# One short row of biases in DRAM, three output blocks at once on the arriving input, and dummy products in front

## The chip, the cores and the metric

The kernel runs on one core of one Trainium2 chip. The metric is the time of one execution on the device, in microseconds, lower is better; a kernel's time is the median of its runs. TensorE (PE in the profile) multiplies matrices, VectorE (DVE), ScalarE (ACT) and GpSimd (POOL) do the rest, SyncE (SP) issues most transfers.

## The reference

A trunk of two layers on x of 256 tokens by 2048 features, all in float32. Each layer is a mixer and a feed-forward part, each behind an rmsnorm and added to x.

```python
def swa_sink_attention(q, k, v, sinks, rel_bias):        # layer 0, 8 heads, window 128
    mask, bias = banded_mask_bias(rel_bias, A_WINDOW, nb)   # bias = rel_bias[t5_bucket(dist)]
    logits = einsum('bnqgrd,bnkgd->bgrnqk', qb, kb) * SCALE + bias
    ...
def nsa_attention(...):                                   # layer 1, 8 heads
    ...
    ls = einsum('bqgrd,bgqkd->bgrqk', qi, k_g) * SCALE + bias_s     # selected blocks
    lw = einsum('bqgrd,bkgd->bgrqk', qi, kwi) * SCALE + bias_w      # window 512
```

Beside them layer 0 has a forgetting attention and layer 1 a gated delta net. The bias of a query and a key depends on their distance alone: with 256 tokens each head has one row of at most 384 values per mask, read at another offset for each query.

## The kernel before

Nearly all of the time goes into products of weights with the activations. A weight is split into a high part `wh` (ACT, L168) and a remainder `wl` (DVE or POOL, L169); the activations are kept the same way in `xhl` (`split_x`: ACT at L385, DVE at L386, which multiply by the gain vector `vec`). A block of 128 output features (`f_job`) is 16 pairs of products, one per 128 input features: `wh` with 512 columns (L305) and `wl` with 256 (L306), summed in one PSUM bank. `v_job` gives token-major output, three products per input block and token block (L342 to L344).

Weights arrive as 1 MB loads into three buffers `wf`, issued by SP (L151); each load is cut into two pieces of 8 input blocks. `run` splits two pieces ahead of the products. The fragments of a split are issued in `hook`, which is called after every second pair; the same hook advances the side work, generators that say with `yield n` after how many hooks they go on. So the order of every engine's instructions is fixed by the count of hooks. An output block is taken out of PSUM (`fsum`: a copy at L448, an add at L451, then a product on POOL at L400) once the norm is known (`norm["ready"]`); `room(n)` holds the next job back until at most n results wait for it.

Layer 0 runs these jobs: two key blocks (k0, k1), query blocks q0 to q2, the token-major job V0 (264 columns), q3 to q7, two token-major jobs V1 of 512 columns, then 16 blocks for the other attention, then 32 half blocks for the output projection. `boot` issues the input x (four loads of 512 KB, `hT`), the first weights in two halves of 512 KB and a second load; it splits the input and the first two pieces. `first_gen` squares the input and sums it (L1412 on DVE, L1414 on ACT, L1416 on POOL, L1419 and L1421 on DVE), `norm_gen` turns that into the norm.

`bias_gen` makes the biases of all heads as 8 rows of 384 values with one product (L539), adds a mask in two versions (`brow`, L543) and writes each version 128 times into DRAM, one copy per query, with a row step of 385 (L547); head h then reads a skewed 128x256 table from it (`load_bias`, L555). `a_gen` runs the eight heads of the first attention: it waits for the query block, for V0 and for `state["bias"]`, loads the bias of head 0, waits 8 hooks, and from then on loads each head's bias one head ahead. `head_gen` (L567 to L606) issues the logits, the bias add with the maximum (L577, L578), the exponentials, transposes (L597 to L599) and the last product. `nsa_gen` in layer 1 does the same with three heads side by side, and loads the bias at the start of each head.

Of the kernel before, what the change touches and what calls it, by code (L numbers as in the profile page):

```python
# [48 lines left out]
WS = 3  # L49

# ---------------------------------------------------------------- shape-only constants
# [20 lines left out]
def _consts():  # L72
    p = np.arange(128)
    i64 = np.arange(64)
    j = np.arange(T)
    f = np.float32
    ident = np.eye(128, dtype=f)
    tri = (p[:, None] <= p[None, :]).astype(f)
    causal = np.where(j[None, :] <= 128 + p[:, None], 0.0, NEG).astype(f)
    y = np.arange(384)  # L80
    dist = 255 - y
    onehot = (np.arange(32)[:, None] == _t5_bucket(dist)[None, :]).astype(f)
    mask_a = np.where((dist >= 0) & (dist < 128), 0.0, NEG).astype(f)[None].repeat(8, 0)
    mask_c = np.where(dist >= 0, 0.0, NEG).astype(f)[None].repeat(8, 0)
    c0, o0 = _pack([("ident", ident)])
    c1, o1 = _pack([("tri", tri), ("causal", causal)])
    cb, ob = _pack([("onehot", onehot), ("mask_a", mask_a), ("mask_c", mask_c)])
    pj = p % 64
    blk = (p[:, None] // 64) == (p[None, :] // 64)
    lv, lvt = [], []  # L90
    for s in (1, 2, 4, 8, 16, 32):
        a, b = pj[:, None], i64[None, :]
        same = (a // (2 * s)) == (b // (2 * s))
        lv.append((same & (a % (2 * s) < s) & (b % (2 * s) >= s)).astype(f))
        lvt.append((same & (a % (2 * s) >= s) & (b % (2 * s) < s)).astype(f))
# [30 lines left out]
def trunk(ctx, tc, a, out):  # L126
# [16 lines left out]
    # ------------------------------------------------------------ weight stream  # L143
# [4 lines left out]
    def issue_load(l):  # L148
        src, n = loads[l]
        t = tmp.tile([128, 2048], F32, tag="wf", name="wf", bufs=3)  # L150
        nc.sync.dma_start(t[:, :n], src)  # L151
        wf_tiles[l] = t

    def split(i):
        pc = pieces[i]
        t = wf_tiles[pc["load"]]
        w = t[:, pc["off"]:pc["off"] + pc["n"]]
# [78 lines left out]
    def room(n):  # L236
        """at most n results wait for the norm."""
        while len(pending) > n:
            if norm["ready"]:
                flush()  # L240
            else:
                step_sides()

    def run():
        while state["i"] < len(pieces):
# [8 lines left out]
            if i < 2:  # L254
                settle()
# [6 lines left out]
            if pc["after"]:  # L262
                pending.append(pc["after"])
                flush()
# [11 lines left out]
    def f_job(src, nk, rhs, evac, pre=None, key=None, tag=None, one=False):  # L276
        """128 output features: psum[:, :256] + psum[:, 256:] is the product of src with rhs."""
# [39 lines left out]
    def v_job(src, ncol, xs, evac, pre=None):  # L317
        """token-major output [128 tokens, ncol] for the two token blocks."""
# [34 lines left out]
    # ------------------------------------------------------------ constants  # L353
# [26 lines left out]
    # ------------------------------------------------------------ norms  # L380
# [24 lines left out]
    def rsqrt(y, v, n, it=3):  # L405
        """y = v ** -0.5 on a [128, n] tile."""
# [66 lines left out]
    def to_out(k):  # L473
        """the last residual: its gained value goes to the output buffer, to be scaled by the norm."""
# [34 lines left out]
    def softplus(x, n, name):  # L509
        """log(1 + exp(x)) on a [128, n] tile."""  # L510
# [18 lines left out]
    # ------------------------------------------------------------ bias rows  # L529
# [4 lines left out]
    scr = [dram.tile([8, 128 * 385], F32, name=f"scr{q}") for q in range(2)]  # L534

    def bias_gen():
        yield 6
# [6 lines left out]
        for q in range(2):  # L544
            yield 4
            r = scr[q]
            nc.scalar.dma_start(bass.AP(tensor=r.tensor, offset=r.offset, ap=[[128 * 385, 8], [385, 128], [1, 384]]),  # L547
                                brow[q][:, None, :].to_broadcast([8, 128, 384]))
            yield 16
            state["bias"] = True  # L550

    def load_bias(q, h, tag):
        t = tmp.tile([128, T], F32, tag=tag, name="bias", bufs=1)
        r = scr[q]
        nc.scalar.dma_start(t, bass.AP(tensor=r.tensor, offset=r.offset + h * 128 * 385 + 127,  # L555
                                      ap=[[384, 128], [1, T]]))
        return t

    # ------------------------------------------------------------ attention of one head, two query blocks
# [3 lines left out]
    def head_gen(h, tags, u, q, k, v, add1, add0, oT, extra=None, sink=None):  # L563
        """softmax attention of head h; q, k: [128 d, 256]; v: two [128 keys, 128 d] blocks."""
# [44 lines left out]
    # ------------------------------------------------------------ layer 0 mixer  # L609
    def even_mixer():  # L610
# [76 lines left out]
        def a_gen():  # L687
            for h in range(8):
# [5 lines left out]
                if h < 7:  # L694
# [4 lines left out]
                                    bias, bias[:, 128:], oA[:, h], sink=sinks[:, h:h + 1])  # L699
# [22 lines left out]
        blk = iter(range(26))  # L722
        for g in range(2):
            f_job(wF[next(blk)], 16, x, ev_k(g))
        for h in range(8):
# [19 lines left out]
    # ------------------------------------------------------------ feed-forward  # L745
# [57 lines left out]
    def start_norm(scaled=False):  # L803
        def f():
            norm["ready"] = False
            side(norm_gen(scaled))
        return f
# [10 lines left out]
    # ------------------------------------------------------------ layer 1 mixer  # L818
    def odd_mixer():
# [100 lines left out]
        # ---- compressed keys and values  # L920
# [73 lines left out]
        # ---- sparse attention  # L994
        def nsa_gen(u, tag, tE, tP, tC, tB):
# [4 lines left out]
            while heads:  # L1000
# [9 lines left out]
                for qb in range(2):  # L1010
# [5 lines left out]
                    add = [bias[:, T - n:], bias[:, T - n:]]  # L1016
# [48 lines left out]
        # ---- gated delta net: head pairs, chunks of 64 tokens, both heads side by side on the partitions  # L1065
# [62 lines left out]
        def inv_gen(p, ta, tb):  # L1128
# [78 lines left out]
            def part(t, h, s):  # L1207
                """columns j of [128, 4, n] with j // s % 2 == h; h None: all of a [128, 4, 32] result."""
# [113 lines left out]
        # ---- jobs  # L1322
# [79 lines left out]
    # ------------------------------------------------------------ the two layers  # L1402
    late = [(c0, a["c0"]), (vec[:, nv:], a["vec"][:, nv:])]
    sqs = [big("t8_0", [128, 8, T], name="sqs"), big("t8_1", [128, 8, T], name="sqs")]

    def first_gen():
        f = lambda t: t.rearrange("p a t -> p (a t)")
        s = [f(sqs[q // 2][:, 4 * (q % 2):4 * (q % 2) + 4]) for q in range(4)]
        for q in range(4):
            h = f(hT[:, 4 * q:4 * q + 4])  # L1410
            if q % 2:
                V.tensor_mul(s[q], h, h)  # L1412
            else:
                A.activation(s[q], h, AF.Square)  # L1414
            if q % 2:
                G.tensor_tensor(s[q - 1], s[q - 1], s[q], op=ALU.add)  # L1416
            yield S1
        yield S2
        V.tensor_add(s[0], s[0], s[2])  # L1419
        yield 2  # L1420
# [3 lines left out]
        yield W0  # L1424
        acc["n"] = KT

    def boot(gi):
        """the input, the first weights and their parts, in the order of their use."""
        src, n = loads[0]
        wf_tiles[0] = t = tmp.tile([128, 2048], F32, tag="wf", name="wf", bufs=3)  # L1430
        state["nl"] = 1
        h = n // 2

        def lx(q):
            nc.sync.dma_start(hT[:, 4 * q:4 * q + 4], a["x"][:, 4 * q:4 * q + 4])

        def sx(q):
            for k in range(4 * q, 4 * q + 4):
                split_x(k, gi)

        lx(0)
        nc.sync.dma_start(t[:, :h], src[:, :h])
        lx(1)
        lx(2)
        nc.sync.dma_start(t[:, h:n], src[:, h:n])
        lx(3)
        issue_load(1)
        state["nl"] = 2
        for d, s in late:
            nc.sync.dma_start(d, s)  # L1450
        sx(0)
        split(0)
        settle()
        sx(1)
        sx(2)
        split(1)
        settle()
        sx(3)
# [4 lines left out]
    start_norm(True)()  # L1463
# [33 lines left out]
def _fblk(w):  # L1497
    """[K, N] -> [N / 128, 128, K / 128, 128], partitions first."""
# [66 lines left out]
```

## Time and profile before

| | |
|---|---|
| time, median of 3 runs | 2418.19 us (2416.05 to 2419.87) |
| profiled execution, span of core 0 | 2420.8 us |
| its time outside the span | not given; the span is 2.6 us over the median |
| TensorE busy | 2351.2 us, 97% |
| DVE, ACT, POOL busy | 66%, 55%, 27% |
| DMA | 425.00 MB, mean 176 GB/s |

TensorE is busy when a product is in its pipeline; how fast it goes depends on the clock that it is granted (PEclk), which has two levels, 1.2 and 2.4 GHz, shown as 0.50 and 1.00. Idle time of another engine counts only where TensorE waits for it.

### The profile page before, as it was taken

What the parts mean: (1) busy time and instruction counts of PE and PEld (TensorE: products, weight loads), DVE (VectorE), ACT (ScalarE), POOL (GpSimd) and SP (SyncE); (2) the same over time, 40 slices, a digit from 0 to 9 for tenths busy, and PEclk for the clock granted to TensorE, in tenths of its full rate; (3) what the DMA queues carried; (4) which work ended last, traced back from release to release, by engine and by line L of the source; (5) the groups of instructions that cost most, each with busy time, mean ns of one, the idle gap of its engine ahead of it and who ended that gap; (6) DMA issues with size and microseconds to landing.
All of it is one profiled execution on the core that took longest, in us unless ns stands there. A gap on an engine that the chain in (4) does not pass through costs nothing.

```text
span 2420.8 us, 40042 instructions
## 1 busy us (share of the span) xinstructions
PE 2351.2 (97%) x14374; PEld 2032.6 (84%) x14374; DVE 1595.0 (66%) x3454; ACT 1337.5 (55%) x3377; POOL 660.1 (27%) x926
## 2 busy tenths in 40 slices
PE   7799999999999999999999999999999999999997
PEld 5688888888888888888777777887888888888887
DVE  6457687666656666667887756778666655666654
ACT  4355566555545555555655445666555544555553
POOL 1223353111121111233444433345111121111132
PEclk9899999999999999999999999999999999999999
DMA  7554355555556555555433454345555556555554
GB/s 202 166 186 152 119 173 191 184 193 190 178 189 207 192 184 194 177 190 190 165 123 112 151 182 174 105 151 191 192 188 194 168 189 201 192 190 192 176 192 137
DMA packets 74358, 425.00 MB, mean 176 GB/s; under 512 B 8336, under 2 KB 12944, under 8 KB 31792
## 3 DMA queue, kind: packets, MB, share of 16 engines
q1 hardware_dynamic: 68544, 415.14, 50.2%
q10 hardware_dynamic: 5616, 7.32, 1.6%
q8 instruction: 113, 1.85, 0.3%
q14 instruction: 85, 0.70, 0.1%
HBM read 417.18 MB, written 5.24 MB: 174 GB/s over the span
## 4 chain that ended last, share of the span: by engine, by line
PE 83%; DVE 4%; issue 4%; POOL 4%; DMA 3%; ACT 2%; POOLq 0%; SPq 0%; DVEq 0%; ACTq 0%
PE mm L305 49%; PE mm L306 25%; POOL wl L169 2%; DVE wl L169 1%; DMA wf<-in_w_evF_dram 1%; PE s L1205 1%; DMA bias<-scr 1%; PE mm L342 1%; PE mm L343 1%; PE mm L344 1%; ACT wh L168 1%; DMA wf<-in_w_evV_dram 1%; POOL acc L403 1%; POOL hT L460 1%; PE s L1058 1%
## 5 line engine op out<-in xcount | busy, mean ns | idle before, releaser
L169 DVE TENSOR_TENSOR wl<-wf,wh 128x512 fp32r<-128x512 f32 (+4 forms) x1833 | 1105.6, 625 | 686.0 <-ACT wh L168 672.2
L305 PE MATMUL mm<-xhl,wh 128*128 128x512 f32 x3968 | 1418.6, 398 | 21.9 <-ACT wh L168 17.9
L168 ACT CAST wh<-wf 128x512 fp32r<-128x512 f32 (+2 forms) x2064 | 964.1, 510 | 423.1 <-PE mm L305 338.9
L306 PE MATMUL mm<-xhl,wl 128*128 128x256 f32 x3968 | 1124.0, 283 | 4.7 <-DVE wl L169 4.7
L305 PEld LDWEIGHTS mm<-xhl,wh 128*128 128x128 f32 x3968 | 751.3, 189 | 192.6 <-ACT wh L168 19.1
L306 PEld LDWEIGHTS mm<-xhl,wl 128*128 128x128 f32 x3968 | 756.2, 191 | 9.3 <-DVE wl L169 7.1
L305 PE MATMUL mm<-hid,wh 128*128 128x512 f32 x1386 | 482.1, 392 | 0.0
L306 PE MATMUL mm<-hid,wl 128*128 128x256 f32 x1386 | 388.5, 280 | 0.0
L400 POOL TENSOR_TENSOR gp<-ta,rbc 128x256 f32<-128x256 f32 x112 | 116.4, 1039 | 716.6 <-DVE ta L451 704.9
L305 PEld LDWEIGHTS mm<-hid,wh 128*128 128x128 f32 x1386 | 260.1, 188 | 58.4 <-DVE hid L507 1.2
L306 PEld LDWEIGHTS mm<-hid,wl 128*128 128x128 f32 x1386 | 260.7, 188 | 0.0
L448 ACT COPY tb<-mm 128x256 f32<-128x256 f32 x287 | 106.6, 372 | 265.0 <-PE mm L306 237.9
L169 POOL TENSOR_TENSOR wl<-wf,wh 128x256 fp32r<-128x256 f32 (+3 forms) x231 | 187.3, 812 | 172.9 <-ACT wh L168 154.7
L400 POOL TENSOR_TENSOR u<-u,cv 128x256 f32<-128x256 f32 x88 | 65.3, 742 | 212.5 <-ACT cv L783 212.5
L451 DVE TENSOR_TENSOR ta<-mm,tb 128x256 f32<-128x256 f32 x287 | 119.6, 417 | 1.7 <-ACT tb L448 1.7
L460 POOL TENSOR_TENSOR hT<-hT,ta 128x256 f32<-128x256 f32 x91 | 72.4, 796 | 81.6 <-DVE ta L451 64.1
L459 POOL TENSOR_TENSOR ta<-ta,rbc 128x256 f32<-128x256 f32 x39 | 38.2, 980 | 178.8 <-DVE ta L451 178.8
L403 POOL TENSOR_TENSOR acc<-acc,sq 128x256 f32<-128x256 f32 x59 | 52.3, 886 | 58.3 <-ACT sq L395 58.3
L783 ACT ACTIVATE cv<-cv 128x256 f32<-128x256 f32 x88 | 36.8, 419 | 55.5 <-DVE cv L781 55.5
L767 DVE TENSOR_TENSOR u<-mm,tb 128x256 f32<-128x256 f32 x88 | 37.5, 426 | 39.2 <-ACT tb L765 39.2
L342 PE MATMUL mm<-wh,xhl 128*128 128x512 f32 (+3 forms) x160 | 54.6, 341 | 6.4 <-ACT wh L168 6.4
L344 PE MATMUL mm<-wl,xhl 128*128 128x512 f32 (+3 forms) x160 | 54.1, 338 | 0.0
(353 smaller groups left out, 2048.5 us busy)
## 6 DMA issues: line engine op xcount, KB each, us to landing
wf<-in_w_up_dram SPq DMA_DIRECT2D x176, 1024.0 KB, 4.8
wf<-in_w_dn_dram SPq DMA_DIRECT2D x64, 1024.0 KB, 4.9
wf<-in_w_odF_dram SPq DMA_DIRECT2D x48, 1024.0 KB, 4.9
wf<-in_w_evF_dram SPq DMA_DIRECT2D x25, 1024.0 KB, 4.9
wf<-in_w_dn_dram SPq DMA_DIRECT2D x64, 384.0 KB, 3.1
wf<-in_w_evO_dram SPq DMA_DIRECT2D x32, 512.0 KB, 3.6
wf<-in_w_odO_dram SPq DMA_DIRECT2D x32, 512.0 KB, 3.6
wf<-in_w_evV_dram SPq DMA_DIRECT2D x8, 1024.0 KB, 4.9
```

Source lines behind the costliest of these rows:

```text
L168: A.copy(wh[:, c], w[:, c])
L169: e.tensor_tensor(wl[:, c], w[:, c], wh[:, c].bitcast(F32), op=ALU.subtract)
L305: P.matmul(ps, wh[:, c], xb.rearrange("p a t -> p (a t)"), start=k == 0, stop=False)
L306: P.matmul(ps[:, 256:512], wl[:, c], xb[:, 0, :], start=False, stop=k == nk - 1)
L342: P.matmul(ps, xh, wh[:, c], start=k == 0, stop=False)
L344: P.matmul(ps, xh, wl[:, c], start=False, stop=k == KT - 1)
L400: G.tensor_tensor(out, x, y, op=ALU.mult)
L403: G.tensor_tensor(out, x, y, op=ALU.add)
L448: A.copy(tb, ps[:, T:2 * T])
L451: V.tensor_tensor(t, ps[:, :T], tb, op=ALU.add)
L459: e.tensor_tensor(t, t, R["bc"], op=ALU.mult)
L460: e.tensor_tensor(hT[:, k], hT[:, k], t, op=ALU.add)
```

## The change

The bias rows are made in reverse order (`dist[::-1]`) and written once per version, 8 x 384 values. A head's load reads 128 overlapping rows of 256 values, each one value further on, and the bias is read backwards by DVE (`last_keys`, a step of -1). `bias_gen` starts at hook 34 instead of 6, and `state["bias"]` is set after both writes.

The first three blocks, k0, k1 and q0, are computed together (`boot_job`): eight pieces, each of two input blocks times three output blocks, in three PSUM banks. Input and weights come in five steps of x and the three blocks' weights (first two of 256 and 384 KB, then three of 512 and 768 KB); the fourth chunk of weights has a buffer of its own (`wf3`). Each piece splits its two input blocks and three weight parts, the middle one's remainder on POOL, two pieces ahead. There is a hook after every two pairs, so 24 in these jobs, as before.

`first_gen` now squares two quarters of the input on POOL (hooks 9 and 14), one on ACT and one on DVE, and adds on DVE alone. The norm waits 3 and 6 hooks where it waited 4 and 8. Nine products of `ones` with itself stand ahead of everything on TensorE. `room` now flushes and advances the side work in every round.

```diff
+WARM = 9
     dist = 255 - y
+    dist = dist[::-1]
 def issue_load(l):
     src, n = loads[l]
+        if callable(src):
+            wf_tiles[l] = src()
+            return
 def split(i):
+        if "parts" in pc:
+            ...
+            for k in pc["rows"]:
+                frags.append(lambda k=k: split_x(k, 0))
+            for o, c, n, e in pc["parts"]:
+                def piece(o=o, c=c, n=n, e=e):
+                    A.copy(wh[:, c:c + n], t[:, o:o + n])
+                    e.tensor_tensor(wl[:, c:c + n], t[:, o:o + n], wh[:, c:c + n].bitcast(F32), op=ALU.subtract)
+                frags.append(piece)
 def room(n):
         while len(pending) > n:
-            if norm["ready"]:
-                flush()
-            else:
-                step_sides()
+            flush()
+            step_sides()
 def run():
-            if i < 2:
-                settle()
+    def boot_job(src, evacs, rhs, bring):
+        box = {}
+        nb = len(evacs)
+        for c in range(4):
+            loads.append((lambda c=c: bring(c), nb * 512))
+            for q in range(2):
+                def mm(wh, wl, c=c, q=q):
+                    if c == q == 0:
+                        box["ps"] = [psm.tile([128, 512], F32, tag="mm", name="mm") for _ in range(nb)]
+                    for j in range(nb):
+                        ps = box["ps"][j]
+                        for r in range(2):
+                            k = 4 * c + 2 * q + r
+                            w = slice((2 * j + r) * 128, (2 * j + r + 1) * 128)
+                            xb = rhs(k)
+                            P.matmul(ps, wh[:, w], xb.rearrange("p a t -> p (a t)"), start=k == 0, stop=False)
+                            P.matmul(ps[:, 256:512], wl[:, w], xb[:, 0, :], start=False, stop=k == KT - 1)
+                        hook()
+                last = c == 3 and q == 1
+                add_piece(len(loads) - 1, 0, nb * 256, mm,
+                          [lambda j=j: start(evacs[j], box["ps"][j], None) for j in range(nb)] if last else None)
+                pieces[-1]["rows"] = range(4 * c + 2 * q, 4 * c + 2 * q + 2)
+                pieces[-1]["parts"] = [(j * 512 + q * 256, j * 256, 256, G if j == 1 else V) for j in range(nb)]
-    scr = [dram.tile([8, 128 * 385], F32, name=f"scr{q}") for q in range(2)]
+    scr = [dram.tile([8, 384], F32, name=f"scr{q}") for q in range(2)]
 def bias_gen():
-        yield 6
+        yield 34
         for q in range(2):
             yield 4
-            nc.scalar.dma_start(bass.AP(tensor=r.tensor, offset=r.offset, ap=[[128 * 385, 8], [385, 128], [1, 384]]),
-                                brow[q][:, None, :].to_broadcast([8, 128, 384]))
-            yield 16
-            state["bias"] = True
+            nc.scalar.dma_start(scr[q], brow[q])
+        yield 16
+        state["bias"] = True
 def load_bias(q, h, tag):
-        nc.scalar.dma_start(t, bass.AP(tensor=r.tensor, offset=r.offset + h * 128 * 385 + 127,
-                                      ap=[[384, 128], [1, T]]))
+        nc.scalar.dma_start(t, bass.AP(tensor=r.tensor, offset=r.offset + h * 384 + 1, ap=[[1, 128], [1, T]]))
+    def last_keys(t, n):
+        return bass.AP(tensor=t.tensor, offset=t.offset + n - 1, ap=[t.ap[0], [-1, n]])
 def a_gen():
-                                    bias, bias[:, 128:], oA[:, h], sink=sinks[:, h:h + 1])
+                                    last_keys(bias, T), last_keys(bias, 128), oA[:, h], sink=sinks[:, h:h + 1])
-        for g in range(2):
-            f_job(wF[next(blk)], 16, x, ev_k(g))
-        for h in range(8):
+        boot_job(wF[0:3], [ev_k(0), ev_k(1), ev_q(0)], lambda k: xhl[:, k], lambda c: bring(c, wF))
+        for h in range(1, 8):
 def nsa_gen(u, tag, tE, tP, tC, tB):
-                    add = [bias[:, T - n:], bias[:, T - n:]]
+                    add = [last_keys(bias, n), last_keys(bias, n)]
 def first_gen():
-        for q in range(4):
-            ...
+        yield 8
+        gmul(s[0], h(0), h(0))
+        yield 5
+        gmul(s[1], h(1), h(1))
+        yield 5
+        A.activation(s[2], h(2), AF.Square)
+        yield 4
+        V.tensor_add(s[0], s[0], s[1])
+        yield 2
+        V.tensor_mul(s[3], h(3), h(3))
+        yield 1
+        V.tensor_add(s[2], s[2], s[3])
+        yield 1
         V.tensor_add(s[0], s[0], s[2])
-        yield 2
+        yield 1
         V.tensor_add(s[0][:, 0:512], s[0][:, 0:512], s[0][:, 512:1024])
         V.tensor_add(acc["t"], s[0][:, 0:256], s[0][:, 256:512])
-        yield W0
+        yield 1
+    def bring(c, src):
+        ...
+        for q in range(2) if c == 0 else (None,):
+            k, n = (4 * c, 4) if q is None else (2 * q, 2)
+            nc.sync.dma_start(hT[:, k:k + n], a["x"][:, k:k + n])
+            nc.sync.dma_start(w[:, :, (k % 4) * 128:(k % 4 + n) * 128],
+                              src[0:3, :, k:k + n, :].rearrange("j p k c -> p j (k c)"))
 def boot(gi):
-        ...
+        dummy = bank("s4")
+        for _ in range(WARM):
+            P.matmul(dummy[:, 0:128], ones, ones, start=True, stop=True)
+        for c in range(4):
+            issue_load(c)
         for d, s in late:
             nc.sync.dma_start(d, s)
+        state["nl"] = 4
+        for i in range(2):
+            split(i)
+            settle()
         state["ns"] = 2
-    start_norm(True)()
+    start_norm(True, 3)()
```

## Rows read from the trace of the kernel before

**Rows 1.** The page: the span, and one line of the DMA issues

```profile
span 2420.8 us, 40042 instructions
...
wf<-in_w_evF_dram SPq DMA_DIRECT2D x25, 1024.0 KB, 4.9
```

**Rows 2.** Busy time in two stretches; columns: PE, PEld, DVE, ACT, POOL, clock, DMA share, GB/s

```profile
0.00:120.00 120.00, 85.39 (x442) 73.31 (x443) 66.66 (x181) 52.07 (x159) 24.77 (x36) 0.87 0.66 185
120.00:2420.80 2300.80, 2265.77 (x13934) 1959.32 (x13932) 1528.38 (x3274) 1285.46 (x3218) 635.29 (x890) 0.99 0.51 175
```

**Rows 3.** The chain that ended last, 0 to 160 us; columns: start, us, what

```profile
32.41 18.76 DMA wf<-in_w_evV_dram
...
56.76 19.03 DMA wf<-in_w_evF_dram
...
78.91 19.55 DMA bias<-scr
```

**Rows 4.** DMA issues up to 200 us, and landings of the bias loads

```profile
scr<-brow ACTq DMA_DIRECT2D x2, 1536.0 KB
...
DMA to landing us min/median/max: 2.0/3.0/19.6
```

**Rows 5.** Busy time in a stretch of the first long load

```profile
46.00:53.00 7.00, 0.73 (x5) 0.37 (x3) 1.03 (x3) 0.92 (x4) 0.51 (x1) 0.90 0.50 168
```

**Rows 6.** Timeline of PE; in brackets the idle time before and what ended it

```profile
8.90 0.79 PE L305 MATMUL mm<-xhl,wh 128*128 128x512 f32 x1 [8.90 <-ACT wh L168]
...
14.07 0.40 PE L305 MATMUL mm<-xhl,wh 128*128 128x512 f32 x1
...
17.49 0.81 PE L539 MATMUL s<-cb,rb 32*8 32x384 f32 x2
...
20.30 0.28 PE L306 MATMUL mm<-xhl,wl 128*128 128x256 f32 x1
...
20.64 0.28 PE L306 MATMUL mm<-xhl,wl 128*128 128x256 f32 x1
...
53.11 0.59 PE L342 MATMUL mm<-wh,xhl 128*128 128x264 f32 x1 [6.39 <-ACT wh L168]
...
76.35 0.80 PE L305 MATMUL mm<-xhl,wh 128*128 128x512 f32 x1 [8.97 <-ACT wh L168]
...
103.74 0.48 PE L597 MATMUL s<-c,E 128*128 128x128 f32 x1 [7.48 <-DVE E L594]
...
120.62 0.40 PE L342 MATMUL mm<-wh,xhl 128*128 128x512 f32 x1
```

**Rows 7.** Timeline of ACT, DVE and POOL, start of the kernel

```profile
5.05 1.71 ACT L385 ACTIVATE xhl<-hT,vec 128x256 fp32r<-128x256 f32 x4 [2.37 <-DMA vec<-in_vec_dram]
...
8.45 1.32 ACT L168 CAST wh<-wf 128x256 fp32r<-128x256 f32 x4 [1.69 <-DMA wf<-in_w_evF_dram]
...
14.67 1.43 DVE L169 TENSOR_TENSOR wl<-wf,wh 128x256 fp32r<-128x256 f32 x4
...
16.01 1.67 DVE L386 SCALAR_TENSOR_TENSOR xhl<-hT,vec,xhl 128x256 fp32r<-128x256 f32 x4
...
20.23 3.64 DVE L169 TENSOR_TENSOR wl<-wf,wh 128x256 fp32r<-128x256 f32 x4
...
20.47 2.45 POOL L1416 TENSOR_TENSOR sqs<-sqs 128x1024 f32<-128x1024 f32 x1 [18.20 <-DVE sqs L1412]
...
76.73 0.74 POOL L169 TENSOR_TENSOR wl<-wf,wh 128x256 fp32r<-128x256 f32 x1 [13.72 <-ACT wh L168]
```

**Rows 8.** Busy time in stretches of 2 us after the waits

```profile
58.00:60.00 2.00, 2.00 (x17) 2.00 (x17) 1.95 (x5) 0.39 (x2) 0.90 (x2) 0.90 0.73 131
...
82.00:84.00 2.00, 2.00 (x12) 1.69 (x11) 1.76 (x8) 1.14 (x4) 0.94 (x2) 0.93 0.91 229
...
108.00:110.00 2.00, 2.00 (x8) 1.71 (x7) 0.71 (x2) 0.22 (x1) 1.21 (x2) 0.60 0.92 381
```

**Rows 9.** Timeline of DVE, an add over 1024 columns

```profile
29.11 1.20 DVE L1419 TENSOR_TENSOR sqs<-sqs 128x1024 f32<-128x1024 f32 x1
```

More of the change, by code (lines that the diff above doesn't have):

```diff
@@ L156, in split @@
         t = wf_tiles[pc["load"]]
+        if "parts" in pc:
+            wh = tmp.tile([128, 1024], F32R, tag="wh", name="wh", bufs=NW)
+            wl = tmp.tile([128, 1024], F32R, tag="wl", name="wl", bufs=NW)
+            for k in pc["rows"]:
[5 more added lines that the diff above has]
+                frags.append(piece)
+            sp_tiles[i] = (wh, wl)
+            return
         w = t[:, pc["off"]:pc["off"] + pc["n"]]
@@ L261, in run @@
             settle()
-            if pc["after"]:
-                pending.append(pc["after"])
-                flush()
+            for fn in pc["after"] if isinstance(pc["after"], list) else [pc["after"]]:
+                if fn:
+                    pending.append(fn)
+                    flush()
             state["i"] += 1
@@ L545, in bias_gen @@
             yield 4
-            r = scr[q]
-            nc.scalar.dma_start(bass.AP(tensor=r.tensor, offset=r.offset, ap=[[128 * 385, 8], [385, 128], [1, 384]]),
-                                brow[q][:, None, :].to_broadcast([8, 128, 384]))
-            yield 16
-            state["bias"] = True
+            nc.scalar.dma_start(scr[q], brow[q])
+        yield 16
+        state["bias"] = True
     def load_bias(q, h, tag):
@@ L721, in even_mixer @@
         wF, wV0, wV1 = a["w_evF"], a["w_evV0"], a["w_evV1"]
-        blk = iter(range(26))
-        for g in range(2):
-            f_job(wF[next(blk)], 16, x, ev_k(g))
-        for h in range(8):
+        blk = iter(range(3, 26))
+        boot_job(wF[0:3], [ev_k(0), ev_k(1), ev_q(0)], lambda k: xhl[:, k], lambda c: bring(c, wF))
+        for h in range(1, 8):
             f_job(wF[next(blk)], 16, x, ev_q(h), tag={1: "s2", 2: "s3"}.get(h))
@@ L801, in ffn, with start_norm @@
                           to_res(n, gi_next if half else "none", True), key=("x", n) if half else None)
-    def start_norm(scaled=False):
+    def start_norm(scaled=False, w=4):
         def f():
             norm["ready"] = False
-            side(norm_gen(scaled))
+            side(norm_gen(scaled, w))
         return f
@@ L1403, in trunk @@
     late = [(c0, a["c0"]), (vec[:, nv:], a["vec"][:, nv:])]
+    wf3 = big("t8_2", [128, 2048], name="wf3")
     sqs = [big("t8_0", [128, 8, T], name="sqs"), big("t8_1", [128, 8, T], name="sqs")]
@@ L1408, in first_gen @@
         s = [f(sqs[q // 2][:, 4 * (q % 2):4 * (q % 2) + 4]) for q in range(4)]
-        for q in range(4):
[L1410 to L1418, printed above, removed]
+        h = lambda q: f(hT[:, 4 * q:4 * q + 4])
+        yield 8
[11 more added lines that the diff above has]
+        yield 1
         V.tensor_add(s[0], s[0], s[2])
-        yield 2
+        yield 1
         V.tensor_add(s[0][:, 0:512], s[0][:, 0:512], s[0][:, 512:1024])
@@ L1423, in first_gen @@
         V.tensor_add(acc["t"], s[0][:, 0:256], s[0][:, 256:512])
-        yield W0
+        yield 1
         acc["n"] = KT
-    def boot(gi):
[L1429 to L1448, printed above, removed]
+    def bring(c, src):
+        if c < 3:
+            t = tmp.tile([128, 2048], F32, tag="wf", name="wf", bufs=3)
+        else:
+            t = wf3
+        w = t[:, 0:1536].rearrange("p (j x) -> p j x", j=3)
+        for q in range(2) if c == 0 else (None,):
[3 more added lines that the diff above has]
+                              src[0:3, :, k:k + n, :].rearrange("j p k c -> p j (k c)"))
+        return t
+    def boot(gi):
+        dummy = bank("s4")
[3 more added lines that the diff above has]
+            issue_load(c)
         for d, s in late:
             nc.sync.dma_start(d, s)
[L1451 to L1458, printed above, removed]
+        state["nl"] = 4
+        for i in range(2):
+            split(i)
+            settle()
         state["ns"] = 2
```

## The prediction

> **What bounds the kernel now.** I read the page, then the busy time in stretches, because a share over 2421 us hides where the idle time lies. After 120 us TensorE is busy 2265.77 of 2300.8 us; before it only 85.39 of 120 [rows 2]. So the change, which touches the start and the bias rows, can win from these 34.6 us of idle time and from slow clock in the same stretch; the rest is bound by TensorE. The chain that ended last, cut to the start, names the holes: a weight load of 18.76 us, another of 19.03 us and a bias load of 19.55 us [rows 3], where a 1024 KB weight load usually lands in 4.9 us [rows 1]. During the first of these holes the DMA engines are half busy and move 168 GB/s [rows 5]. What runs then is the pair of scratch writes, 1536 KB each out of 8 partitions [rows 4]. The timeline of TensorE shows what the holes cost: it starts at 8.90, waits 6.39 us before 53.11 (the job V0, 264 columns for two token blocks), 8.97 us before 76.35 (the fourth query block) and 7.48 us before 103.74 (the transposes of head 0, which had waited for its bias) [rows 6]. After each wait the clock is at its lower level: its mean is 0.90 in 58 to 60, 0.93 in 82 to 84 and 0.60 in 108 to 110, so the engine came back to the upper level at about 58.4, 82.3 and 109.6 [rows 8].
>
> I therefore use one mark: the first product of the next job, V1 (512 columns), at 120.62 [rows 6]. What V1 gains, the end gains, since TensorE is never short of work for long behind it.
>
> **From V0 to V1.** 120.62 - 53.11 = 67.5 us. Take off the two waits, 8.97 + 7.48 = 16.5. Take off half of the slow stretches (a step at the lower level takes twice as long): (5.3 + 5.9 + 5.9) / 2 = 8.5. 42.6 us of work remain. This holds after the change if the scratch writes no longer delay weights and head 0's bias is in time.
>
> **The scratch rows.** The 3 MB of writes become two of 12 KB; their cost goes to nothing and so does what they held up. New: one bias load reads 128 overlapping rows of 1 KB from the same 1.5 KB of DRAM. The trace has no such load. Nearest is the load of today: 2.0 us at best, 3.0 at the median, 19.6 under the writes [rows 4]; I take 3.0 and keep 2.0 and 19.6. In layer 0 it is hidden: the flag comes at slot 58 (34 + 4 + 4 + 16; a slot is the break between products in which side work is issued), the load is issued in that slot, head 0 starts 11 slots on and adds the bias 2 slots after, 13 slots of two pairs of products, 13 x 2 x 0.34 = 8.8 us [rows 6]. Later heads load a whole head ahead. The ACT queue, on which the load waits for the scratch write, is held for nothing: 16 slots lie between. Head 0 starts at slot 58 today (V0 ends at slot 46), then at 69; heads take 20 slots, so head 7 ends at about 225 where it ended at 214, still ahead of slot 230, where the output projection would drain it. If that cover were gone, the rest of one head, a few us, would be exposed. The reversed read of the bias is in no row. Nearest is a DVE operation of 256 columns, 0.36 us (1.43 / 4 [rows 7]); a head adds bias to 256 and 128 columns, so about 0.5 us, and at half speed 0.5 more, 4 us for eight heads were all of it exposed. I take 0, because DVE has room where the heads run, and see no way to a gain.
>
> **The start.** Today TensorE begins at 8.90, at the lower level until about 14 [rows 6]. After the change the gain vector still comes at 5.05 and sets the start [rows 7], unless the first 640 KB are later. Two splits on ScalarE (1.71 / 4 = 0.43 each) and one weight copy (1.32 / 4 = 0.33) later, TensorE starts at 5.05 + 0.86 + 0.33 = 6.2 [rows 7]. The three blocks are 48 pairs, a pair 20.64 - 20.30 = 0.34 us [rows 6], so 16.3 us. The lower end of their finish is 6.2 + 16.3 = 22.5.
>
> The upper end comes from DVE and POOL. For each of the eight pieces (two rows of input, three blocks) DVE makes two splits (1.67 / 4 = 0.42) and two remainders (1.43 / 4 = 0.36), POOL one remainder (0.74), and POOL gets two squares of 128x1024, for which the nearest row is today's sum of 2.45 us [rows 7]. While that sum ran, from 20.47, four DVE remainders took 3.64 us instead of 1.43 [rows 7]: DVE stood still. If they never overlap, this is 8 x (0.84 + 0.72 + 0.74) + 4.9 = 23.3 us, from 5.5 (5.05 + 0.43) to 28.8, and a last product of 0.7: 29.5. The trace shows the collision for the long operation; that short ones alternate without loss I do not know, and buffers let DVE run two pieces ahead. I take the middle, 26.0, and keep 22.5 and 29.5.
>
> The Trainium skill, "SBUF — State Buffer", section "Who interferes with whom", says that a DVE instruction with two SBUF inputs and a GpSimd instruction that reads SBUF exclude each other for a whole instruction. It speaks against squares on POOL in this place. By it the three blocks would end at 29.5, by the row on free DVE work alone (8 x 1.56 = 12.5 us) TensorE would set 22.5; here the one row of the collision, 3.64 us for 1.43, agrees with it.
>
> Data: weights of 512 KB landed only at 8.45 today [rows 7], the new first part is 384 KB of them behind 256 KB of input. At best it is no later than the vector; at worst it lands at 8.45, some 2.5 us late. I take 0 and keep 2.5. The nine dummy products cost nothing, since TensorE has no work before 6.2; if they lift the clock they save up to half of 8.90 to 14, 2.5 us. I charge half of that, 1.2, and keep 0 and 2.5.
>
> **Up to V0.** Two more query blocks: 32 x 0.34 = 10.9. The one-hot product, 0.81 [rows 6], and the norm's two small steps, taken as the same again: 1.6. The norm stands at slots 32 and 38: DVE must have four operations of 1.2 us [rows 9] and half that again behind, about 5.8 us, and eight to twelve weight remainders of 0.36 done while TensorE works 5.4 us; 5.8 + 3.6 = 9.4 leaves up to 4 us uncovered, less what DVE is ahead. I take 2 (0 to 4). V0 needs two PSUM buffers whose contents wait for the norm: two copies and two adds, 1.5 (1 to 2).
>
> **The sum.** V0 starts at 26.0 + 10.9 + 1.6 + 2 + 1.5 + 1.2 = 43.2, V1 at 43.2 + 42.6 = 85.8, which is 34.8 us earlier. Best: 22.5 + 10.9 + 1.6 + 0 + 1 + 0 = 36.0, V1 at 78.6, 42.0 earlier. Worst, with half of the late data still hidden: 29.5 + 1.3 + 10.9 + 1.6 + 4 + 2 + 2.5 = 51.8, V1 at 94.4, 26.2 earlier. The profiled span is 2420.8 [rows 1], 2.6 over the median of the timed runs, 2418.19; I take the saving off the median: **2383.4**.
>
> **Rivals.**
> (A) DVE and POOL get out of each other's way and TensorE alone sets the start: 42.0 us saved, 2376.2. For it: DVE is two pieces ahead. Against: the 3.64 us [rows 7].
> (B) DVE and POOL exclude each other throughout, and the first weights are late: 26.2 saved, 2392.0. For it: the same row; each square holds DVE for 2.45 us while TensorE has two pieces in hand, 6 pairs or 2.04 us each. Against: short operations may fit between. The rule of the Trainium skill named above, "SBUF — State Buffer", section "Who interferes with whom", is this rival's.
> (C) The change doesn't do what it says: weights were late for another cause than the scratch writes. Then V0 still waits to about 50 and the holes stay; saved are the 2.7 us of earlier start and at most 2.5 of clock, 5.2: 2413.0. Against: half-busy engines beside two 1536 KB writes, and 4.9 us loads everywhere else [rows 1, 4, 5].
> (D) Slower: overlapping rows out of one spot of DRAM are slow. In layer 1 each head loads its bias just before use, eight heads in three chains, so three loads in line on the longest. At the 19.6 us once seen, 16.6 over the median, that is 3 x 16.6 = 50 us lost against 34.8 won: 2433. It decides from 34.8 / 3 = 11.6 us more per load. Nothing in the trace speaks for it but the unknown access.
>
> **How the numbers follow.** Forecast 0.45 (its own range 2379 to 2388), A 0.27, B 0.21, C 0.05, D 0.02. The range runs from A, with some us for runs and for side work that falls otherwise, to B: 2375 to 2393 leaves out C and D and a part of A and B, about 0.2. Slower or faster by less than 0.2%, 4.8 us, can hardly be told from no change. Faster needs 2413.4: the forecast, A, B and half of C, 0.96; same 0.02, slower 0.02.
>
> **What would show it.** Right: V0 near 43, V1 near 86 with TensorE at the upper level throughout from 14 on; no load over 10 us after 20 us; DVE remainders stretched to over 2 us beside the two POOL squares; no wait at head 0's transposes. Wrong: long loads in 30 to 80 still (C); bias loads well over 3 us (D); a TensorE wait before the norm's product of more than 4 us, or a clock that falls there again, which would cost beyond B; head 7 drained in front of the output projection.

## The result, and the profile after

| | before | after |
|---|---|---|
| median of the timed runs, us | 2417.12 (2412.07 to 2419.87, 4 runs) | 2391.38 (2389.32 to 2396.0, 4 runs) |
| ratio, 95% interval | | 0.9893 (0.9875 to 0.9912) |
| span of the profiled run, us | 2420.8 | 2389.2 (2391.01 with what lies outside) |
| V0 starts | 53.11 | 48.0 |
| V1 starts | 120.62 | 91.14 |

The change makes the kernel faster by 25.7 us. The measured 2391.38 is 8.0 us over the forecast of 2383.4, inside the range and next to rival B's 2392.0.

The page of the kernel after: the span and the weight loads, against [rows 1].

```profile
span 2389.2 us, 40119 instructions
...
wf<-in_w_evF_dram SPq DMA_DIRECT2D x23, 1024.0 KB, 5.2
```

Busy time in stretches, the columns as in [rows 2].

```profile
0.00:120.00 120.00, 111.26 (x584) 94.45 (x585) 84.59 (x206) 66.89 (x202) 40.88 (x57) 0.96 0.61 203
120.00:2389.20 2269.20, 2235.24 (x13809) 1935.47 (x13807) 1514.35 (x3239) 1269.17 (x3175) 624.52 (x879) 1.00 0.52 175
...
8.00:12.00 4.00, 4.00 (x13) 3.27 (x14) 3.23 (x7) 3.05 (x9) 1.46 (x2) 0.57 1.04 379
...
22.00:24.00 2.00, 2.00 (x7) 1.41 (x7) 2.00 (x3) 0.08 (x1) 1.57 (x2) 0.50 0.98 410
...
40.00:42.00 2.00, 2.00 (x8) 1.71 (x7) 1.69 (x12) 0.00 (x0) 0.00 (x0) 0.50 0.68 165
```

In the first 120 us TensorE is idle for 8.7 us where it was idle for 34.6 [rows 2]; 4.05 us of its busy time there are the dummy products. Behind 120 us its idle time is 34.0 where it was 35.0, so the gain in idle time lies in front, as forecast. The clock is at its lower level in three places (0.57, 0.50, 0.50).

DMA issues up to 200 us, and the landings of all bias loads, against [rows 3, 4].

```profile
wf<-in_w_evV_dram SPq DMA_DIRECT2D x2, 792.0 KB, 4.5
...
scr<-brow ACTq DMA_DIRECT2D x2, 12.0 KB
...
DMA to landing us min/median/max: 2.9/3.3/6.7
```

The long holes are gone: V0's weights land in 4.5 us where the chain had 18.76, and no bias load takes more than 6.7 where one took 19.6.

The timeline of TensorE, in brackets the idle time before and what ended it, against [rows 6].

```profile
0.99 4.05 PE L1492 MATMUL s<-ones 128*128 128x128 f32 x18 [0.99 <-POOL ones L404]
...
7.91 0.61 PE L384 MATMUL mm<-xhl,wh 128*128 128x512 f32 x1 [2.88 <-ACT wh L169]
...
10.68 0.63 PE L384 MATMUL mm<-xhl,wh 128*128 128x512 f32 x1
...
19.36 0.47 PE L384 MATMUL mm<-xhl,wh 128*128 128x512 f32 x1 [0.85 <-ACT wh L169]
...
21.00 0.38 PE L385 MATMUL mm<-xhl,wl 128*128 128x256 f32 x1 [1.18 <-DVE wl L170]
...
31.02 0.39 PE L319 MATMUL s<-xhl,wh 128*128 128x512 f32 x1
...
38.34 0.58 PE L469 MATMUL s<-ones,acc 128*128 128x1 f32 x4 [1.61 <-DVE acc L1470]
38.78 0.69 PE L319 MATMUL s<-xhl,wh 128*128 128x512 f32 x1
...
42.60 0.81 PE L580 MATMUL s<-cb,rb 32*8 32x384 f32 x2
...
48.00 0.36 PE L356 MATMUL mm<-wh,xhl 128*128 128x264 f32 x1 [0.70 <-DVE ta L492]
...
91.14 0.40 PE L356 MATMUL mm<-wh,xhl 128*128 128x512 f32 x1
```

The nine dummies, 18 rows in this view, end at 5.04, the first real product comes at 7.91, the three blocks end at 31.02, and the row at 38.34 waits for the sum of squares. From V0 to V1 it takes 43.1 us, and none of the long waits of [rows 6] is left there.

The timeline of ACT, DVE and POOL, against [rows 7].

```profile
7.45 1.02 ACT L169 CAST wh<-wf 128x256 fp32r<-128x256 f32 x3 [1.44 <-DMA wf<-in_w_evF_dram]
...
16.86 2.07 POOL L441 TENSOR_TENSOR sqs<-hT 128x1024 f32<-128x1024 f32 x1
...
17.10 2.98 DVE L427 SCALAR_TENSOR_TENSOR xhl<-hT,vec,xhl 128x256 fp32r<-128x256 f32 x2
...
20.00 2.97 DVE L170 TENSOR_TENSOR wl<-wf,wh 128x256 fp32r<-128x256 f32 x2
...
20.63 2.07 POOL L441 TENSOR_TENSOR sqs<-hT 128x1024 f32<-128x1024 f32 x1
```

Each square of POOL stretches a pair of DVE operations to 2.98 and 2.97 us, which take 0.88 and 0.75 elsewhere in this trace. In the first pair one operation alone lasts from 17.10 to 19.21, as long as POOL's square beside it. TensorE's wait to 19.36 ends just behind that, though its row names ACT, and the wait to 21.00 ends with the next remainder of DVE, begun at 20.00. TensorE's clock falls behind this second wait.

### The profile page after: what moved, and what is told of

It reads as the page before. It is cut to its first block, busy times and chain, and to the rows that moved or that the text cites. A ratio compares the mean times of both kernels' runs of the same rounds, so it can differ in the third digit from the quotient of the medians.

```text
span 2389.2 us, 40119 instructions
## 1 busy us (share of the span) xinstructions
PE 2346.5 (98%) x14392; PEld 2029.9 (85%) x14392; DVE 1598.9 (67%) x3445; ACT 1336.1 (56%) x3376; POOL 665.4 (28%) x936
## 4 chain that ended last, share of the span: by engine, by line
PE 86%; DVE 4%; POOL 4%; issue 3%; ACT 2%; DMA 1%; POOLq 0%; DVEq 0%; ACTq 0%
PE mm L319 50%; PE mm L320 26%; POOL wl L186 1%; DVE wl L186 1%; PE s L1247 1%; PE mm L356 1%; PE mm L357 1%; PE mm L358 1%; POOL acc L444 1%; ACT wh L185 1%; POOL hT L501 1%; PE s L1100 1%; DMA wf<-in_w_evF_dram 0%; DVE cv L1128 0%; PE s L1056 0%
## 5 line engine op out<-in xcount | busy, mean ns | idle before, releaser
L319 PE MATMUL mm<-xhl,wh 128*128 128x512 f32 x3920 | 1392.8, 397 | 3.9 <-DVE xhl L427 3.9
L185 ACT CAST wh<-wf 128x512 fp32r<-128x512 f32 (+3 forms) x2040 | 956.7, 511 | 401.9 <-PE mm L319 337.5
L320 PE MATMUL mm<-xhl,wl 128*128 128x256 f32 x3920 | 1106.1, 282 | 2.5 <-DVE wl L186 2.5
L319 PEld LDWEIGHTS mm<-xhl,wh 128*128 128x128 f32 x3920 | 737.7, 188 | 169.3 <-issue 9.2
L320 PEld LDWEIGHTS mm<-xhl,wl 128*128 128x128 f32 x3920 | 742.8, 189 | 5.6 <-DVE wl L186 3.4
L821 ACT ACTIVATE cv<-gp,vec 128x256 f32<-128x256 f32 x88 | 53.0, 603 | 0.0
```

The costliest lines, as they stand in the source:

```text
L185: A.copy(wh[:, c], w[:, c])
L319: P.matmul(ps, wh[:, c], xb.rearrange("p a t -> p (a t)"), start=k == 0, stop=False)
L320: P.matmul(ps[:, 256:512], wl[:, c], xb[:, 0, :], start=False, stop=k == nk - 1)
L821: A.activation(c, gp[:, 2:T + 2], AF.Identity, scale=cw(2), bias=vc("fcb", l * HT + j))
```

## The experiments

Two questions were put: which half of the change brings the gain, and why the start brings less than forecast. Each kernel stands against runs of the kernel before on the same chip; its saving is the difference of those medians. Not all kernels ran on one chip, so where two of them are compared, the difference of their medians stands beside the one by their ratios.

**rows_only**: the kernel before with the short reversed rows alone. The lines show the writes; the reversal and the reads are those of the change.

```diff
-            r = scr[q]
-            nc.scalar.dma_start(bass.AP(..., ap=[[128 * 385, 8], [385, 128], [1, 384]]),
-                                brow[q][:, None, :].to_broadcast([8, 128, 384]))
-            yield 16
-            state["bias"] = True
+            nc.scalar.dma_start(scr[q], brow[q])
+        yield 16
+        state["bias"] = True
```

> The kernel before with the short reversed bias rows alone (hook 6 as before, old start). Theory 1 (nearly all of the gain is the scratch writes that no longer delay weights): the three long loads go to about 5 us, V0 starts at about 47 (q2 ended at 46.7 before), V1 at 47 + 43 = 90, so 25 to 31 us saved, 0.987 to 0.990, as much as the whole change. Theory 2 (the new start carries a good part): 15 to 20 us saved, 0.992 to 0.994. Theory 3 (the overlapping rows are slow to read): bias loads land far over 3.3 us.

Measured: 2389.57 (2388.11 to 2390.22, 4 runs), ratio 0.9882 (0.9868 to 0.9895), 28.7 us saved. That is the whole gain. The timeline of TensorE, V0 and V1:

```profile
46.59 0.29 PE L343 MATMUL mm<-wh,xhl 128*128 128x264 f32 x1
...
90.05 0.40 PE L343 MATMUL mm<-wh,xhl 128*128 128x512 f32 x1
```

Busy time where the first long load of before lay [rows 5]:

```profile
46.00:53.00 7.00, 7.00 (x58) 6.92 (x57) 6.30 (x16) 3.67 (x13) 2.92 (x4) 1.00 0.58 176
```

With the old start V0 begins even 1.4 us sooner than in the kernel after, and TensorE is never idle in a stretch where it worked 0.73 of 7 us in the kernel before [rows 5].

**start_only**: the kernel after with the skewed tables put back, written at slot 10.

```diff
-    scr = [dram.tile([8, 384], F32, name=f"scr{q}") for q in range(2)]
+    scr = [dram.tile([8, 128 * 385], F32, name=f"scr{q}") for q in range(2)]
-        yield 34
+        yield 6
-            nc.scalar.dma_start(scr[q], brow[q])
+            (write, wait and read as in the kernel before)
```

> The changed kernel with the old skewed table of biases (written at hook 10 and 30, 3 MB) and the old reads: the new start alone. Theory 1: the long loads come back, 0 to 6 us saved, 0.9975 to 1.000. Theory 2: 8 to 15 us saved, 0.994 to 0.997.

Measured: 2416.47 (2412.89 to 2421.04, 12 runs), ratio 0.9993 (0.9983 to 1.0003): nothing. V0 came at 62.34, later than in the kernel before. Who waited, with the times (total, count, longest):

```profile
ACT wh L184 <- DMA scr<-brow: 21.4, 1, 21.4
```

ScalarE stood for 21.4 us in front of its weight copies for a table write. So this kernel's V0 is not the price of the new start alone; that is read from the kernel after against rows_only, which differ in the start and run at 0.9893 and 0.9882.

**two_writes** and **one_write**: rows_only, and with it writes of the old form into DRAM that nothing reads: two (20 slots apart, as before), or one. The edit of two_writes:

```diff
+    scrx = [dram.tile([8, 128 * 385], F32, name=f"scrx{q}") for q in range(2)]
...
             nc.scalar.dma_start(scr[q], brow[q])
-        yield 16
-        state["bias"] = True
+            r = scrx[q]
+            nc.scalar.dma_start(bass.AP(tensor=r.tensor, offset=r.offset, ap=[[128 * 385, 8], [385, 128], [1, 384]]),
+                                brow[q][:, None, :].to_broadcast([8, 128, 384]))
+            yield 16
+            state["bias"] = True
```

> The kernel with the short rows alone, plus, behind each short write, one write of brow to a table of 1536 KB out of 8 partitions that nobody reads: the same two writes as before at the same places, but no load waits for their data. Theory 1 (they hurt through the engines that they share with the weights): weight loads of 15 to 19 us come back and most of the 28.7 us is lost again: 2408 to 2418. Theory 2 (the time went into waiting for the table, which only the bias loads need): within 4 us of the short rows alone, 2386 to 2394.

> The kernel one_write that ran held one extra write of 1536 KB, not two; this one holds both, one behind each short write and 20 slots apart as before, into tables that nobody reads. One extra write cost 9.2 us against the short rows alone (2398.8 against 2389.6). Theory 1 (they hurt through the engines that they share with weights, and the second more than the first because the weights in hand are used up by then): 2405 to 2418, with weight loads of 15 us and more until about 95 us. Theory 2 (two cost twice one, and the rest of the 28.7 us was the biases' wait for the table): 2404 or less is not reached from above, 2406 to 2409 with no wait at head 0. Theory 3 (only the wait for the table matters beyond the first write): 2397 to 2401.

The one_write that ran held one unread write in all, behind both short ones, not one behind each as its expectation has it. Measured: one_write 2398.79 (2395.71 to 2403.24, 6 runs), ratio 0.9927 (0.9912 to 0.9942), 9.2 us over rows_only (10.9 by the ratios); two_writes 2417.64 (2414.3 to 2421.24, 11 runs), ratio 1.0001 (0.9992 to 1.001), 28.1 over rows_only (28.8 by the ratios). The chain of two_writes, against [rows 3]:

```profile
32.50 18.84 DMA wf<-in_w_evV_dram
...
56.93 18.90 DMA wf<-in_w_evF_dram
...
78.96 19.90 DMA bias<-scr
```

Its busy time in the stretch of [rows 5]:

```profile
46.00:53.00 7.00, 0.00 (x0) 0.00 (x0) 1.03 (x3) 0.76 (x3) 0.34 (x1) 0.79 0.50 168
```

The three links of before are back to within 0.4 us, with the half-busy engines and the 168 GB/s, though nobody reads what is written; the bias loads here read the short rows. So the gain is these two writes and nothing else of the tables. The two are not alike. The timeline of TensorE in one_write shows the only long wait between 40 us and V1:

```profile
52.41 0.59 PE L343 MATMUL mm<-wh,xhl 128*128 128x264 f32 x1 [7.78 <-ACT wh L169]
```

One write delays V0's weights and costs 9 to 11 us; the second brings the waits for the fourth query block and for head 0's bias, another 18 to 19. That bias load is issued on the queue of the writes, so whether it came late by its turn behind them or by the engines that they share is not shown. What SP's queue waits for in two_writes says more on it:

```profile
SPq L152 <- DMA scrx<-brow: 18.1, 2, 17.8
```

A weight load was not even issued until a write had landed with which it shares no data. The kernel before has the same wait (16.3 us), one_write and rows_only wait for no write. What ties the load to the write was not tested and stays open.

**wide_write**: the kernel before, its tables of the same 1536 KB, each written out of 128 partitions with 8 copies instead of 8 with 128.

```diff
-            nc.scalar.dma_start(bass.AP(..., ap=[[128 * 385, 8], [385, 128], [1, 384]]),
-                                brow[q][:, None, :].to_broadcast([8, 128, 384]))
+            nc.scalar.dma_start(bass.AP(..., ap=[[8 * 385, 128], [385, 8], [1, 384]]),
+                                brow[q][:, None, :].to_broadcast([128, 8, 384]))
```

The one-hot product then gives each row 16 times over (`rx`, a copy of `rb` by DVE). `bias_gen` starts 4 slots later here, and the masks are loaded for all 128 partitions.

> The kernel before, skewed tables and old start kept, with each table (the same 1536 KB) written out of 128 partitions (each head's row made on 16 of them, 8 copies each) instead of out of 8 (128 copies each); hook 10 instead of 6, and masks for all 128 partitions loaded. Theory 1 (the harm is that a write out of 8 partitions holds half of the DMA engines at a low rate for 20 to 30 us): each write lands in 4 to 8 us, no weight load over 10 us after 40 us, and 20 to 28 us are saved though the bytes are all there, 0.988 to 0.992. Theory 2 (the harm is the bytes written to DRAM beside the weights): long loads stay, 0.996 to 1.000.

Measured: 2395.62 (2393.61 to 2401.91, 5 runs), ratio 0.9918 (0.9904 to 0.9931), 22 us saved with all bytes still written. Its DMA issues up to 200 us:

```profile
scr<-brow ACTq DMA_DIRECT2D x2, 1536.0 KB, 11.5
wf<-in_w_evV_dram SPq DMA_DIRECT2D x2, 792.0 KB, 7.8
```

Its timeline of TensorE has a wait of its own, for the copies of `rb`:

```profile
27.52 1.64 PE L541 MATMUL s<-cb,rx 32*128 32x384 f32 x2 [7.80 <-DVE rx L540]
```

So it is the form of the write more than its bytes. V0's weights need 7.8 us beside it, where the chain had 18.76. How much of the 6 us to rows_only (8.7 by the ratios) is the bytes and how much the 7.80 us is open.

**no_dummies** (`WARM = 0`) and **warm_16** (`WARM = 16`, from 9), else the kernel after.

> The changed kernel with no dummy products. They end at 5.0 and the first product starts at 7.91 at the lower clock level all the same, so Theory 1: no change, within 1 us of the changed kernel. Theory 2 (they bring the clock up sooner): 2 to 3 us slower than the changed kernel, with the lower level lasting beyond 12 us.

> The changed kernel with 16 dummy products instead of 9, so that they end at about 7.5, just ahead of the first real product. Theory 1 (the start is bound by data and by DVE, not by the clock): the lower level at 8.2 to 11.6 goes, but the time stays within 1 us of the changed kernel. Theory 2: 1.5 to 3 us faster.

Measured: no_dummies 2390.11 (2389.07 to 2390.49, 4 runs), ratio 0.9883 (0.9867 to 0.9899); warm_16 2388.48 (2387.35 to 2391.43, 4 runs), ratio 0.9886 (0.9872 to 0.9899). By their ratios neither can be told from after (0.9893). The timeline of no_dummies:

```profile
7.29 0.79 PE L384 MATMUL mm<-xhl,wh 128*128 128x512 f32 x1 [7.29 <-ACT wh L169]
...
10.05 0.63 PE L384 MATMUL mm<-xhl,wh 128*128 128x512 f32 x1
...
11.16 0.40 PE L384 MATMUL mm<-xhl,wh 128*128 128x512 f32 x1
```

Its slow products, 0.63 us for 0.40, last until 10.7, those of the kernel after until 11.3: the nine dummies did not bring the upper level forward. The clock column is no help here, it reads 1.00 in no_dummies from 8 to 12.

The timeline of warm_16:

```profile
0.99 6.46 PE L1492 MATMUL s<-ones 128*128 128x128 f32 x32 [0.99 <-POOL ones L404]
...
7.95 0.50 PE L384 MATMUL mm<-xhl,wh 128*128 128x512 f32 x1 [0.50 <-ACT wh L169]
```

And its busy time from there:

```profile
8.00:12.00 4.00, 4.00 (x19) 3.04 (x20) 3.32 (x7) 3.13 (x9) 1.47 (x2) 1.00 1.06 381
12.00:24.00 12.00, 8.59 (x43) 6.21 (x42) 10.80 (x14) 9.25 (x28) 8.38 (x7) 1.00 1.04 404
```

With 32 rows of dummies and no long gap behind them the clock stays at the upper level (19 products in 8 to 12 for 13 in the kernel after, none of 0.63 us). But TensorE then waits 3.4 of the 12 us from 12 on: it only comes sooner to what it has to wait for, and V0 starts at 46.17, where no_dummies has 47.35.

**squares_act**: the kernel after, its two squares of POOL on ScalarE.

```diff
-        gmul(s[0], h(0), h(0))
+        A.activation(s[0], h(0), AF.Square)
...
-        gmul(s[1], h(1), h(1))
+        A.activation(s[1], h(1), AF.Square)
```

> The changed kernel with the two early squares of 128x1024 on ScalarE instead of POOL, in the same places. Theory 1 (each square on POOL holds DVE for its length): no DVE remainder or split over 1 us before 28 us, TensorE doesn't wait at 19 to 21 and its clock does not fall at 22; the three blocks end at 27 to 28 instead of 31.0, 3 to 5 us faster than the changed kernel. Theory 2 (the start is bound by ScalarE or by the arrival of data): no faster, ends at 31 or later.

Measured: 2392.0 (2387.88 to 2393.17, 4 runs), ratio 0.9889 (0.9874 to 0.9904). A row of DVE's timeline:

```profile
17.18 0.87 DVE L427 SCALAR_TENSOR_TENSOR xhl<-hT,vec,xhl 128x256 fp32r<-128x256 f32 x2
```

The collision is gone (0.87 for 2.98), with it both waits of TensorE in the three blocks; its timeline of TensorE:

```profile
8.01 0.79 PE L384 MATMUL mm<-xhl,wh 128*128 128x512 f32 x1 [2.81 <-ACT wh L169]
...
27.37 0.39 PE L319 MATMUL s<-xhl,wh 128*128 128x512 f32 x1
...
36.08 0.58 PE L469 MATMUL s<-ones,acc 128*128 128x1 f32 x4 [3.00 <-DVE acc L1470]
```

The blocks end at 27.37, 3.65 us before after's 31.02, and the norm's product comes 2.3 us sooner. But it now waits 3.00 us for the sum of squares, where it waited 1.61, and the clock is at 0.50 from 38 to 44 behind that; V0 starts at 47.28, and the time is the same.

**norm_later**: squares_act, and the norm's first product 3 slots later, its second step and the bias row's slots moved with it. **norm_quiet**: the same, and three small loads of ACT's queue (`row`, `cb`, `rb`) behind the first weights on SP. **all_act**: the same, the fourth square on ScalarE too, and `WARM = 11`.

```diff
-    start_norm(True, 3)()
+    start_norm(True, 6, 3)()
...
-        yield 34
+        yield 42
...
-    nc.scalar.dma_start(cb[:32], a["cb"][:32])
+    defer.append((cb[:32], a["cb"][:32]))
...
-        V.tensor_mul(s[3], h(3), h(3))
+        A.activation(s[3], h(3), AF.Square)
```

> The changed kernel with the two early squares on ScalarE, the norm's first product 3 slots later (slot 35, transposes at 38 as before) and the bias product behind the norm (slot 42, with 8 instead of 16 slots after the writes, so the flag comes at 58 as before). Theory 1 (with the squares off POOL the sum of squares on DVE is what TensorE waits for, and the clock that falls there): the wait of 3.0 us in front of the norm's product goes under 1 us, no lower clock level after 12 us, V0 starts at 41 to 44 instead of 47 to 48, 3 to 6 us faster than the changed kernel. Theory 2: the wait only moves to the transposes or to V0's buffers, within 1.5 us of the changed kernel.

> The same, and the three small loads on the ScalarE queue that are not needed at once (row, cb, rb) go to the end of the start's SP loads. Theory 1 (small transfers in front of the first weights delay them): the first weights land by 6.5 instead of 7.4 to 7.9, first product at about 6.5, another 1 to 2 us. Theory 2 (the first weights are late by their own many 1 KB rows): first product still at 7.5 to 8, no difference from the kernel without it.

> norm_quiet with the fourth square on ScalarE too and 11 dummy products. Theory 1 (the sum of squares on DVE is what TensorE still waits for before the norm, 1.7 us and a lower clock level from 35 to 39): the wait goes under 0.8 us and the lower level goes, V0 starts at 39.5 to 41 instead of 42.1, 1 to 2.5 us off norm_quiet. Theory 2: ScalarE with four squares becomes the bound of the start: no faster, TensorE waits for xhl or wh before 30 us.

Measured: norm_later 2388.76 (2385.95 to 2389.39), ratio 0.9882 (0.9867 to 0.9897); norm_quiet 2387.39 (2386.08 to 2388.38), 0.9879 (0.9866 to 0.9893); all_act 2385.75 (2383.76 to 2386.17), 0.9872 (0.9857 to 0.9887), four runs each. The timeline of norm_later:

```profile
35.94 0.58 PE L469 MATMUL s<-ones,acc 128*128 128x1 f32 x4 [1.07 <-DVE acc L1470]
...
43.19 0.36 PE L356 MATMUL mm<-wh,xhl 128*128 128x264 f32 x1 [0.70 <-DVE ta L492]
```

The timeline of norm_quiet:

```profile
5.76 0.49 PE L384 MATMUL mm<-xhl,wh 128*128 128x512 f32 x1 [0.81 <-ACT wh L169]
...
42.08 0.36 PE L356 MATMUL mm<-wh,xhl 128*128 128x264 f32 x1 [0.70 <-DVE ta L492]
```

The timeline of all_act:

```profile
5.66 0.50 PE L384 MATMUL mm<-xhl,wh 128*128 128x512 f32 x1 [0.20 <-ACT wh L169]
...
33.19 0.58 PE L469 MATMUL s<-ones,acc 128*128 128x1 f32 x4 [0.50 <-DVE acc L1470]
...
37.95 0.40 PE L477 MATMUL s<-c,rcol 128*128 128x128 f32 x2 [1.99 <-issue]
...
40.44 0.56 PE L356 MATMUL mm<-wh,xhl 128*128 128x264 f32 x1
...
85.08 0.40 PE L356 MATMUL mm<-wh,xhl 128*128 128x512 f32 x1
```

V0 moves from 48.0 to 43.19, 42.08 and 40.44 once the waits are taken away together. Not all of them went: in all_act the norm's second step still comes 1.99 us late, and the clock is at its lower level again behind it (0.50 in 40 to 42), which its expectation had denied. all_act's V1 at 85.08 is where the forecast had it (85.8), and its median is 5.6 us under that of after (5.1 by the ratios) and 3.8 under rows_only's (2.4), with no overlap of their runs; they ran on different chips, and the intervals of the ratios overlap in part, so the gain over rows_only is not clear of the noise.

## Why the prediction was right or wrong

**The scratch writes** were rightly named: rows_only has the whole gain, two_writes gives it all back. Rival C is refuted.

**V0 to V1** was forecast at 42.6 us (its terms give 42.5) and took 43.1. Taking the waits and half of the slow stretches off the old time was sound.

**The failed step: the start.** The three blocks were to end at 26.0; they ended at 31.02, just past the far bound (29.5, and 1.3 for late data: 30.8). All that stands behind it in the sum, 10.9 + 1.6 + 2 + 1.5 + 1.2 = 17.2, measured 17.0 (48.0 - 31.02). That is in part luck: the last 1.2, meant for the slow clock at the beginning, belongs ahead of it, and in its place six pairs behind the norm's product took 3.8 us (38.78 to 42.60) for 6 x 0.34 = 2.0, a slow stretch that the sum did not have. Of the 5.0 us, 3.65 are DVE beside POOL, since squares_act, without the two squares on POOL, ends the blocks at 27.37: I had taken the middle between taking turns and no collision, and each square did hold DVE for about 2 us, by which TensorE waited 0.85 and 1.18 and then lost the upper clock. Of the other 1.4 the first product is the cause that can be named: it came at 7.91 for 6.2, because the weights landed at 7.45; norm_quiet, without three small loads ahead of them, starts at 5.76. Both belong to rival B; its V0 of 51.8 was too late by 3.8, and that the time landed beside its 2392.0 owes as much to the base of the saving, below. The 26.0 was the middle of a range and no sum, so this split goes by runs and not by its terms. The Trainium skill, "SBUF — State Buffer", section "Who interferes with whom", says that a DVE instruction with two SBUF inputs contends with a GpSimd instruction that reads SBUF; the trace agrees with 2.98 us for 0.88.

**Behind it, a premise that fell:** that an earlier start adds to the gain. Rows_only, with the old start, has V0 at 46.59, 6.5 us sooner than before, which is about the wait of 6.39 for its weights; to this the forecast, with V0 at 43.2, had the new start add 3.4. It added nothing: V0 came at 48.0. What one hold gives back the next takes (squares_act: 1.61 us of waiting became 3.00). So it is worth nothing as written; with the waits removed together it may be worth 2.4 to 3.8 us (all_act against rows_only, by ratios and by medians).

**The clock** was to be at its upper level from 14 on; it fell at about 22 and 39, each time behind a wait of TensorE. The text had named this at the norm's product as a way to be wrong. The dummies were charged at half of their gain; they gave none (no_dummies).

**The saving was taken off the wrong number.** The profiled run of before, 2420.8 and 1.8 outside by after's row, is 2422.6, so 4.4 over the median of 2418.19 and not 2.6; the other runs of before, 1.9 to 2.5 outside, make it slightly more. Which of its waits were longer than usual the trace cannot say. The balance of the 8.0 us: 5.3 from V1's mark (91.14 for 85.8), 4.4 from this, 0.4 by which after's median lies over its profiled run, less 2.1 won behind V1 that the forecast did not have (31.6 saved by spans, 29.5 at V1). That the end gains what V1 gains thus holds to some us only: rows_only has V1 30.6 us sooner than before and a span 34.2 shorter, all_act has V1 5.0 sooner than rows_only and a span only 2.2 shorter, each from one profiled run.

**The bias rows** held: overlapping rows land in 3.3 us at the median for 3.0 (2.9 to 6.7), head 0 is in time, rival D is refuted. The reversed read costs nothing: DVE's add over 256 columns took 0.411 us at the median, in rows_only, reversed too, 0.424, in the kernel before 0.424. Rival A, with no collision, is refuted by the DVE rows.

## What to carry to other kernels

A DMA that looks cheap on its own queue is to be priced by what it does to the others: look at the DMA share and at who waits while it runs, and put an unread copy of it back to see what it costs. Where several waits of like size follow each other in front of one mark, removing one can be worth nothing until the next is gone, so try them alone and together before the sum of their prices is believed. Dummy products kept the clock up here only where real work followed without a long gap, and saved no time even so, since that work was about to wait for data.

## What the runs showed of the hardware

Two 1536 KB writes out of 8 partitions left the DMA engines half busy (share 0.50, 168 GB/s) and took loads of 0.8 to 1 MB beside them from some 5 us to nearly 19; the same bytes out of 128 partitions landed in 11.5 us a write. The Trainium skill, "DMA: Bandwidth & Descriptors", section "Rules for kernel authors", says that an outermost dimension under 16 confines a DMA to at most that many engines; the share of 0.50 agrees with 8 of 16. That a load's issue can wait for such a write to land (17.8 us) was not expected.
